# The expert stage of a two-block transformer kernel: last units in one pass, output as [token, channel], elementwise work moved off GpSimd

## The chip, the cores and the metric

The kernel runs on one core of a Trainium2 chip. The metric is the device time of one execution in microseconds (us), as the median of the runs. The kernel before takes 3832.88 us, the median of three runs from 3824.02 to 3834.84 us. TensorE (PE, with its weight loads as PEld) does the matmuls, VectorE (DVE), ScalarE (ACT) and GpSimd (POOL) the elementwise work, and SyncE (SP), ACT and POOL start DMAs. Each engine takes its instructions in the order of its own queue.

## The reference

The input has 512 tokens of 1,024 channels, in float32. The first block has two layers of gated feed-forward, token mixing and gated feed-forward again; the second has another token mixing with layer norm, and then a feed-forward of 16,384 experts, which is what the change is about:

```python
def peer_ffn(x, wq, sub_keys, u_tab, v_tab):      # x [512, 1024]
    q = (xf @ wq).reshape(t, 8, 2, 128)           # 8 heads, two half keys each
    scores = einsum("thpc,hpnc->thpn", q, sub_keys)          # 128 keys per half
    s_top, i_top = top_k(scores, 16)
    cand_s = s_top[:, :, 0, :, None] + s_top[:, :, 1, None, :]   # 16 x 16 sums
    best_s, best_pos = top_k(cand_s, 16)          # 16 experts per head and token
    gates = softmax(best_s)
    act = gelu(einsum("cd,chkd->chk", x, u_tab[expert_idx])) * gates
    return einsum("chk,chkd->cd", act, v_tab[expert_idx])

x = layer_norm(ALPHA * x + m, ln1_g, ln1_b)       # ALPHA = 2 ** 0.25
x = layer_norm(ALPHA * x + peer_ffn(x, ...), ln2_g, ln2_b)
```

The expert number is 128 times the index in the first half plus the index in the second. `u_tab` and `v_tab` are two tables of 16,384 rows of 1,024 numbers, 64 MB each.

## The kernel before, in words

Activations lie as eight tiles `x[k]` of [128 channels, 512 tokens]. Every matmul on weights is done with numbers split in a high and a low part in the type fp32r: three products, high by high (L262), high by low (L263) and low by high (L264). A weight unit of 128 x 1,024 floats is loaded by SP (`unit`, L246) into one of four buffers `raw`; ACT rounds it to `wh` (L249), and DVE or POOL subtracts to get `wl` (L250); `wh` and `wl` have three buffers each. `proj` (from L267) runs the eight blocks of a unit one after the other, three products each (`mm3`).

The method `peer` holds the expert stage. It treats the first 128 tokens in another way than the other 384.

- For the first 128 tokens the chosen rows of both tables are fetched. For each of the 128 places (8 heads by 16) POOL starts an indirect DMA (L1733) of one row of `u_tab` per token; DVE multiplies it by the token and sums (L1717). Then one row of `v_tab` per token is fetched, and DVE adds it to `vacc` with its weight (L1725). These are 256 gathers of 0.5 MB, dealt out over the stage by `ROW_STEPS`.
- For the other 384 tokens all experts are computed, 128 units of 128 experts. In stage 1 each unit is a `proj` with `pu`, then gelu on ACT, and the [128, 384] result goes to a buffer `HS` in device memory, with a store from SP (L1787).
- Beside these units runs `route`, dealt out at `ROUTE_STEPS` steps per unit: queries (16 units of `wq`, three of them begun earlier), scores in plain F32 (L1604), the two rounds of top 16 on DVE (`top16`), and `resolve` (equality on DVE, L1573; multiply on POOL, L1576; sum on DVE, L1579). Then for each of six blocks of 64 tokens the gates are spread over all experts by outer products. For four tokens at a time: DVE writes one-hot rows `o1` (L1665) and `o2` (L1667); ACT (four instructions, L1672) and POOL (L1669) scale `o2` with the high and the low part of the gate into `og`; PE multiplies (L1679, 256 columns, two banks for four tokens, from a ring of four banks); ACT copies the high half into `st` (L1683) and DVE adds the low half (L1684). SP stores `st` into a buffer `G`; the last block stays in SBUF.
- In stage 2 each of the 128 units is loaded from `pv`, `HS` and `G`. POOL multiplies activation and gate (`weighted`, L1813 and L1815), ACT and DVE split the product (L257, L258), and PE adds 24 matmuls of 384 columns into eight banks, one per tile of 128 channels.
- At the end `vacc` is added by transposing matmuls, the mean over channels is taken by matmuls with ones, and eight tiles [128 channels, 512 tokens] are stored; the host transposes them.

What sets the order: the code is emitted in program order, except that `issue_after(self.latest)` puts the dealt-out work of routing and rows on each engine right behind the last `wl` on DVE. Each engine's queue is then fixed.

Of the kernel before, what the change touches and what calls it, by code (L numbers as in the profile page):

```python
# [10 lines left out]
F32 = mybir.dt.float32  # L11
# [33 lines left out]
ROWS = 6  # L45


ROUTE_STEPS = 1.65
ROW_STEPS = (1.5, 0.9, 1.0)
# [87 lines left out]
def _layout(inp):  # L137
# [42 lines left out]
    a["ln"] = np.stack([_cols(inp[k][0]) for k in ("ln1_g_2", "ln1_b_2", "ln2_g_2", "ln2_b_2")], 1)  # L180
# [8 lines left out]
class Net:  # L189
    def __init__(self, tc, A, es):  # L190
# [9 lines left out]
        self.evn = 0  # L200
        c = self.const
        self.ident = c.tile([P, P], F32, name="ident")
# [8 lines left out]
        for i in range(2):  # L211
            nc.vector.tensor_copy(self.mdiag[:, i * P:(i + 1) * P], md[:, :P])
        self.x = [c.tile([P, S], F32, name=f"x{k}") for k in range(KT)]

# [272 lines left out]
    def start(self):  # L487
# [17 lines left out]
        self.gain = c.tile([P, DEPTH, 3, KT], F32, name="gain")  # L505

# [1033 lines left out]
    def resolve(self, best, pos, itop, ii, h0, nh):  # L1540
# [27 lines left out]
        for q in range(nh // 2):  # L1568
            for side in range(2):
# [6 lines left out]
                nc.gpsimd.tensor_tensor(e4, e4, it4[:, 2 * q:2 * q + 2, side, None, :].to_broadcast([P, 2, 16, 16]),  # L1576
# [5 lines left out]
    def route(self, X, G, begun):  # L1582
# [53 lines left out]
        for n, (t, a, b) in enumerate(BLOCKS):  # L1636
# [4 lines left out]
            if t not in numbers:  # L1641
# [7 lines left out]
                gh = self.blk(F32R, name="gh")  # L1649
                self.split(tr[:, 2 * P:3 * P], gh[:, :P], gh[:, P:2 * P])  # L1650
                trb = gh[:, 2 * P:].bitcast(BF)[:, :P]
                nc.vector.tensor_copy(trb, tr[:, P:2 * P])
                numbers[t] = tr, gh.bitcast(F32), trb
                yield
            tr, ghf, trb = numbers[t]
# [43 lines left out]

    def four(self, dt, name):  # L1700
        return self.stage.tile([P, 1024], dt, name=name, tag="four", bufs=4)

    def chosen(self, XN, acc):
# [33 lines left out]
        while flying:  # L1737
            land()
            yield True

    def peer(self, out, begun):
        nc, A = self.nc, self.A
        self.next_phase(24, {"A": 3, "S": 1, "T": 4})
# [147 lines left out]
```

## Time and profile before

| | |
|---|---|
| median of the runs | 3832.88 us |
| the profiled execution | 3826.24 us |
| its span | 3824.3 us |
| PE busy | 3582.7 us, 94% |
| DVE busy | 2617.1 us, 68% |
| ACT busy | 1532.2 us, 40% |
| POOL busy | 1162.6 us, 30% |
| DMA | 648.92 MB, mean 170 GB/s |

The span is the time from the first to the last event of one profiled execution, taken with a hardware profiler. Busy times are the union of an engine's instructions; a matmul's record lasts longer than its share of the pipeline, so records overlap. The granted clock (PEclk) is the share of the full clock of 2.4 GHz that PE was given; the other level is 1.2 GHz. Waits are put down to the instruction whose signal came last.

### The profile page before, as it was taken

To read this page: it belongs to the slowest core of one execution; us is meant where nothing else is said; L and a number is where in the kernel's file an instruction comes from. 1 tells how busy PE (TensorE), PEld (TensorE's weight loads), DVE (VectorE), ACT (ScalarE), POOL (GpSimd) and SP (SyncE) were. 2 spreads that over 40 slices of the span, in tenths; PEclk is the share of its full clock that TensorE was granted. 3 is DMA by queue.
4 is the path that set the end of the run, shared out by engine and by line. 5 is a ranking of instruction groups with operands and counts; after the bars stand their busy time and mean duration, and the time that the engine had idled before them with its cause. 6 is when DMAs were issued, how large, how long until landed. Compare 5 with 4: busy or idle time off the path is not lost. (4 is left out here: it accounts for less than half of the span.)

```text
span 3824.3 us, 50711 instructions
## 1 busy us (share of the span) xinstructions
PE 3582.7 (94%) x18689; PEld 3117.3 (82%) x18689; DVE 2617.1 (68%) x4588; ACT 1532.2 (40%) x2751; POOL 1162.6 (30%) x963
## 2 busy tenths in 40 slices
PE   7999999999999999999999989899788888999996
PEld 6888876788888888768888877788788788999996
DVE  6554687655563324876332485689999999999997
ACT  4222366322232223564322353433456466333332
POOL 0000310100010002101000132466676676776664
PEclk9999999999999999999999999999899899999998
DMA  7655320266643333301333222476676777999994
GB/s 244 189 183 184 123 72 12 94 201 190 195 152 99 93 97 104 106 17 45 105 94 93 90 69 70 147 227 220 190 251 236 245 243 255 352 340 341 340 339 141
DMA packets 230329, 648.92 MB, mean 170 GB/s; under 512 B 22784, under 2 KB 80304, under 8 KB 227520
## 3 DMA queue, kind: packets, MB, share of 16 engines
q1 hardware_dynamic: 190592, 506.20, 40.7%
q0 software_dynamic: 39488, 139.48, 10.8%
q8 instruction: 146, 2.39, 0.3%
q14 instruction: 103, 0.84, 0.1%
HBM read 597.36 MB, written 48.23 MB: 169 GB/s over the span
## 5 line engine op out<-in xcount | busy, mean ns | idle before, releaser
L264 PE MATMUL proj<-yh,wl 128*128 128x512 f32 (+2 forms) x3296 | 1208.8, 368 | 55.3 <-DVE wl L250 37.0
L249 ACT ACTIVATE wh<-raw 128x1024 fp32r<-128x1024 f32 (+2 forms) x622 | 648.3, 1043 | 1440.7 <-PE proj L263 793.1
L262 PE MATMUL proj<-yh,wh 128*128 128x512 f32 (+2 forms) x3296 | 1203.9, 370 | 17.4 <-DVE cc L1483 8.8
L263 PE MATMUL proj<-yl,wh 128*128 128x512 f32 (+2 forms) x3296 | 1209.0, 368 | 6.0 <-DVE yl L380 3.4
L250 DVE TENSOR_TENSOR wl<-raw,wh 128x1024 fp32r<-128x1024 f32 (+2 forms) x527 | 708.1, 1345 | 507.3 <-ACT wh L249 500.4
L264 PEld LDWEIGHTS proj<-yh,wl 128*128 128x128 f32 x3296 | 633.1, 192 | 146.9 <-DVE wl L250 45.6
L262 PEld LDWEIGHTS proj<-yh,wh 128*128 128x128 f32 x3296 | 628.7, 193 | 104.6 <-DVE cc L1483 8.9
L263 PEld LDWEIGHTS proj<-yl,wh 128*128 128x128 f32 x3296 | 633.3, 192 | 86.2 <-DVE yl L380 6.5
L393 POOL TENSOR_TENSOR acc<-acc,sq 128x512 f32<-128x512 f32 x32 | 48.9, 1528 | 1545.5 <-ACT sq L392 1176.8
L262 PE MATMUL acc<-yh,wh 128*128 128x384 f32 x1024 | 344.5, 337 | 0.4 <-ACT yh L257 0.4
L263 PE MATMUL acc<-yl,wh 128*128 128x384 f32 x1024 | 344.4, 336 | 0.1
L264 PE MATMUL acc<-yh,wl 128*128 128x384 f32 x1024 | 343.9, 336 | 0.5 <-DVE wl L250 0.5
L262 PE MATMUL proj<-gh,wh 128*128 128x512 f32 (+1 forms) x792 | 294.9, 372 | 1.1 <-ACT wh L249 1.1
L264 PE MATMUL proj<-gh,wl 128*128 128x512 f32 (+1 forms) x792 | 292.7, 370 | 2.5 <-DVE wl L250 2.5
L263 PE MATMUL proj<-gl,wh 128*128 128x512 f32 (+1 forms) x792 | 293.4, 370 | 0.0
L250 POOL TENSOR_TENSOR wl<-raw,wh 128x1024 fp32r<-128x1024 f32 x95 | 239.1, 2519 | 98.3 <-ACT wh L249 97.6
L518 DVE SCALAR_TENSOR_TENSOR scr<-raw,cact 128x1024 bf16<-128x1024 f32 x128 | 156.7, 1225 | 148.0 <-DMA raw<-in_wada 147.4
L1725 DVE SCALAR_TENSOR_TENSOR vacc<-row,act,vacc 128x1024 f32<-128x1024 f32 x127 | 213.5, 1681 | 0.4
L1733 POOL DMA_INDIRECT row<-in_purows,c x128 | 151.1, 1180 | 196.5 <-DVE row L1717 124.7
L1733 POOL DMA_INDIRECT row<-in_pv,c x128 | 149.5, 1168 | 154.6 <-DVE vacc L1725 72.2
L1717 DVE SCALAR_TENSOR_TENSOR row<-row,cact 128x1024 f32<-128x1024 f32 x128 | 187.4, 1480 | 11.7 <-DMA row<-in_purows,c 11.6
L262 PEld LDWEIGHTS acc<-yh,wh 128*128 128x128 f32 x1024 | 192.4, 188 | 1.0 <-ACT yh L257 0.7
(436 smaller groups left out, 5138.3 us busy)
## 6 DMA issues: line engine op xcount, KB each, us to landing
raw<-in_wada SPq DMA_DIRECT2D x144, 512.0 KB
raw<-in_pu SPq DMA_DIRECT2D x128, 512.0 KB
raw<-in_pv SPq DMA_DIRECT2D x128, 512.0 KB
raw<-in_wg SPq DMA_DIRECT2D x84, 512.0 KB
raw<-in_wu SPq DMA_DIRECT2D x84, 512.0 KB
raw<-in_wd SPq DMA_DIRECT2D x64, 512.0 KB
acts<-hg SPq DMA_DIRECT2D x128, 192.0 KB
hs<-acts SPq DMA_DIRECT2D x64, 384.0 KB
```

What stands on the lines that cost most here:

```text
L249: nc.scalar.activation(h[:, :n], raw[:, :n], AF.Copy)
L250: ins = (engine or nc.vector).tensor_sub(l[:, :n], raw[:, :n], h[:, :n].bitcast(F32))
L262: mm(out, lhsT=lh, rhs=rh, start=start, stop=False)
L263: mm(out, lhsT=lh, rhs=rl, start=False, stop=False)
L264: mm(out, lhsT=ll, rhs=rh, start=False, stop=stop)
L393: (engine or nc.vector).tensor_add(acc[:, s], acc[:, s], sq)
L518: nc.vector.scalar_tensor_tensor(scr, raw, 1.0, self.cact, op0=OP.mult, op1=OP.mult, accum_out=self.mod[:, l, j:j + 1])
L1717: nc.vector.scalar_tensor_tensor(row, row, 1.0, XN, op0=OP.mult, op1=OP.mult, accum_out=a)
L1725: nc.vector.scalar_tensor_tensor(acc, row, a, acc, op0=OP.mult, op1=OP.add)
L1733: nc.gpsimd.indirect_dma_start(out=row, out_offset=None, in_=tables[kind], in_offset=bass.IndirectOffsetOnAxis(ap=self.experts[:GT, s:s + ...
```

## The change

- `proj` runs pass by pass: eight products of `wh` with the high parts, eight of `wh` with the low parts, then eight of `wl`.
- All `wl` of the expert units are made by DVE, and the multiply in `resolve` too. POOL keeps the gathers, a few loads and six adds at the end.
- The gates' outer products are plain F32 matmuls of 128 columns, with `og` written by ACT alone; four tokens share one bank, and one ACT instruction copies it out. The low half, its POOL multiply and DVE's add are gone.
- `ROUTE_STEPS` is 2.3 instead of 1.65. Routing ends after 92 units (`kept`), whose activations go to `HS`, now with a store from ACT's queue. The last 36 units are fused: `proj`, gelu, multiply by the gates from `G` (DVE), split, and the second product, one unit behind. The 92 units from `HS` follow, loaded in pairs, multiplied and split 768 wide by DVE.
- The second product takes the activations as the stationary operand and the weights as the moving one, so that it gives [token, channel]: 18 matmuls of 512 columns per unit into six banks.
- The layer norm at the end is done per tile of 128 tokens (`finish`), with sums along the free dimension, and needs x as [token, channel]: 32 transposes instead of 8 (`XT`). The scales `ln2` are loaded as broadcast rows by POOL. The output is stored as [512, 1024].
- `pad` fills the pools in SBUF, so that each begins at a multiple of 512 bytes. `ROWS`, the buffers of gathered rows, is 5 instead of 6, and `ROW_STEPS` deals out other numbers of rows: 75 fall into stage 1, 93 into the fused units and 88 into the late ones, where it was 129 or 130 in stage 1 (124 of them behind 2424 us) and the rest in stage 2.

```diff
-ROUTE_STEPS = 1.65
-ROW_STEPS = (1.5, 0.9, 1.0)
+ROUTE_STEPS = 2.3
+ROW_STEPS = (1.2, 0.8, 2.6, 1.0)
...
+    def pad(self, pool, name, n):
+        self.nc.vector.memset(pool.tile([P, n], F32, name=name, bufs=1), 0.0)
...
-            for k in range(m):
-                xh, xl = X[c + k]
-                s = slice(k * P, (k + 1) * P)
-                self.mm3(ps, h[:, s], l[:, s], xh, xl, c + k == 0, c + k == nk - 1)
+            for i, (w, part) in enumerate(((h, 0), (h, 1), (l, 0))):
+                for k in range(m):
+                    self.nc.tensor.matmul(ps, lhsT=w[:, k * P:(k + 1) * P], rhs=X[c + k][part], start=c + k + i == 0,
+                                          stop=i == 2 and c + k == nk - 1)
...
-                nc.gpsimd.tensor_tensor(e4, e4, it4[:, 2 * q:2 * q + 2, side, None, :].to_broadcast([P, 2, 16, 16]),
+                nc.vector.tensor_tensor(e4, e4, it4[:, 2 * q:2 * q + 2, side, None, :].to_broadcast([P, 2, 16, 16]),
...
-                ot = o2.rearrange("p e t -> p t e")
-                nc.gpsimd.tensor_tensor(og[:, :, 1], ot, ghf[:, P + q:P + q + 4, None].to_broadcast([P, 4, P]),
-                                        op=OP.mult)
                 for i in range(4):
-                    nc.scalar.activation(og[:, i, 0], ot[:, i], AF.Copy, scale=ghf[:, q + i:q + i + 1])
+                    nc.scalar.activation(og[:, i * P:(i + 1) * P], o2[:, :, i], AF.Copy,
+                                         scale=tr[:, 2 * P + q + i:2 * P + q + i + 1])
 
                 def outer(o1=o1, og=og, q=q):
-                    for u in range(2):
-                        ps = self.bank("gp", "T")
-                        for i in range(2):
-                            v = u * 2 + i
-                            nc.tensor.matmul(ps[:, i * 256:(i + 1) * 256], lhsT=o1[:, v * P:(v + 1) * P],
-                                             rhs=og[:, v].rearrange("p a b -> p (a b)"), start=True, stop=True)
-                        p4 = ps.rearrange("p (t x e) -> p e t x", t=2, x=2)
-                        v = q - a + u * 2
-                        nc.scalar.activation(st[:, :, v:v + 2], p4[:, :, :, 0], AF.Copy)
-                        nc.vector.tensor_tensor(st[:, :, v:v + 2], st[:, :, v:v + 2], p4[:, :, :, 1], op=OP.add)
+                    ps = self.bank("gp", "T")
+                    for i in range(4):
+                        c = slice(i * P, (i + 1) * P)
+                        nc.tensor.matmul(ps[:, c], lhsT=o1[:, c], rhs=og[:, c], start=True, stop=True)
+                    nc.scalar.activation(st[:, :, q - a:q - a + 4], ps.rearrange("p (t e) -> p e t", t=4), AF.Copy)
...
+        def second(h, l, hi, lo, end, t):
+            for i, (a, w) in enumerate(((hi, h), (lo, h), (hi, l))):
+                for m in range(2):
+                    q = 2 * t + m
+                    nc.tensor.matmul(acc[q], lhsT=a[:, t * P:(t + 1) * P], rhs=w[:, m * S:(m + 1) * S],
+                                     start=q not in started, stop=end and i == 2)
+                    started.add(q)
...
+        while not over or kept % 2:
+            g = self.t32("hg")[:, GT:]
+            activations(kept, g)
+            nc.scalar.dma_start(HS[kept // 2, :, kept % 2], g)
+            over = over or routed(ROUTE_STEPS)
             gather(ROW_STEPS[self.known == P])
+            kept += 1
...
+        for j in range(kept, NE):
+            if j % 2 == 0:
+                g4 = gates(stage.tile([P, 2 * n], F32, name="gs", tag="gs"), j)
+            hs = self.blk(name="hs")[:, :n]
+            activations(j, hs)
+            nc.vector.tensor_mul(hs.rearrange("p (b t) -> p b t", t=BT), hs.rearrange("p (b t) -> p b t", t=BT),
+                                 g4[:, :, j % 2])
+            hi, lo = (v[:, :n] for v in self.new_pair())
+            self.split(hs, hi, lo)
+            fused.append((*self.unit(A["pv"][:, j]), hi, lo))
+            gather(ROW_STEPS[2])
+            if len(fused) > 1:
+                both(fused.pop(0))
...
+        for j in range(0, kept - 2, 2):
+            for i, hl in enumerate(weighted(j)):
+                both((*self.unit(A["pv"][:, j + i]), *hl))
+                if not self.gathered:
+                    gather(ROW_STEPS[3])
+                    if self.gathered:
+                        finish(0, [vacc[:, :S], vacc[:, S:]])
...
+        for t in range(NT - early):
+            for i, e in enumerate(ends):
+                second(*e, i == 1, t)
+            finish(early + t, acc[2 * t:2 * t + 2])
```

DVE's queue in the middle of the gates, before: `o_...<-pcst,tr` and `o_...<-iota,gh` are the one-hot rows, `st<-st,gp` the add of the low half, `vacc<-row` a gathered row.

```order
L1667 TENSOR_TENSOR o_25934<-iota_19121,gh 128x512
L1667 TENSOR_TENSOR o_25944<-iota_19121,gh 128x512
L250 TENSOR_TENSOR wl<-raw,wh 128x1024
L1725 SCALAR_TENSOR_TENSOR vacc<-row,act,vacc 128x1024 x2
L1667 TENSOR_TENSOR o_25991<-iota_19121,gh 128x512
L1665 TENSOR_TENSOR o_26044<-pcst,tr 128x512
L1684 TENSOR_TENSOR st<-st,gp 128x128x2 x2
L1665 TENSOR_TENSOR o_26064<-pcst,tr 128x512
L1667 TENSOR_TENSOR o_26045<-iota_19121,gh 128x512
L1667 TENSOR_TENSOR o_26065<-iota_19121,gh 128x512
L1684 TENSOR_TENSOR st<-st,gp 128x128x2 x2
L1665 TENSOR_TENSOR o_26121<-pcst,tr 128x512
```

Of each four tokens two adds stand here, among the one-hot rows, the rows and every second unit's `wl` (the others are POOL's).

The same part after (L1674 and L1676 are the one-hot rows, L1724 a row, L259 `wl`):

```order
L1674 TENSOR_TENSOR o_22757<-pcst,tr 128x512
L259 TENSOR_TENSOR wl<-raw,wh 128x1024
L1724 SCALAR_TENSOR_TENSOR vacc<-row,act,vacc 128x1024
L259 TENSOR_TENSOR wl<-raw,wh 128x1024
L1674 TENSOR_TENSOR o_22772<-pcst,tr 128x512
L1674 TENSOR_TENSOR o_22821<-pcst,tr 128x512
L1676 TENSOR_TENSOR o_22822<-iota_19129,tr 128x512
L1676 TENSOR_TENSOR o_22837<-iota_19129,tr 128x512
L1724 SCALAR_TENSOR_TENSOR vacc<-row,act,vacc 128x1024
L1676 TENSOR_TENSOR o_22889<-iota_19129,tr 128x512
L1676 TENSOR_TENSOR o_22904<-iota_19129,tr 128x512
L259 TENSOR_TENSOR wl<-raw,wh 128x1024
```

The adds L1684 have left the queue, and `wl` of the units stands more often in it.

PE's queue at the gates, before:

```order
L264 MATMUL proj<-yh,wl 128x384
L262 MATMUL proj<-yh,wh 128x384
L263 MATMUL proj<-yl,wh 128x384
L264 MATMUL proj<-yh,wl 128x384
L1679 MATMUL gp<-og,o_23778 128x256 x4
L1679 MATMUL gp<-og,o_23835 128x256 x4
L262 MATMUL proj<-yh,wh 128x384
L263 MATMUL proj<-yl,wh 128x384
L264 MATMUL proj<-yh,wl 128x384
L262 MATMUL proj<-yh,wh 128x384
```

The three products alternate, and the outer products stand between two blocks.

And after (L283 is the projection, L1685 the outer products):

```order
L283 MATMUL proj<-yh,wh 128x384 x8
L283 MATMUL proj<-yl,wh 128x384 x8
L283 MATMUL proj<-yh,wh 128x384 x8
L283 MATMUL proj<-yl,wh 128x384 x4
L1685 MATMUL gp<-og,o_22559 128x128 x2
L283 MATMUL proj<-yl,wh 128x384
L1685 MATMUL gp<-og,o_22559 128x128 x2
L283 MATMUL proj<-yl,wh 128x384 x3
L1685 MATMUL gp<-og,o_22568 128x128 x4
L283 MATMUL proj<-yh,wh 128x384 x2
L283 MATMUL proj<-yh,wl 128x384 x8
```

The three products of a block no longer alternate, and the outer products of four tokens, now of 128 columns, stand inside a pass.

PE's queue in the fused units, after; there is no such place before (L1806 is the second product):

```order
L283 MATMUL proj<-yh,wh 128x384 x8
L283 MATMUL proj<-yl,wh 128x384 x8
L283 MATMUL proj<-yh,wl 128x384 x8
L1806 MATMUL acc<-wh,yh 128x512 x2
L1806 MATMUL acc<-wh,yl 128x512 x2
L1806 MATMUL acc<-wl,yh 128x512 x2
L1806 MATMUL acc<-wh,yh 128x512 x2
L1806 MATMUL acc<-wh,yl 128x512 x2
L1806 MATMUL acc<-wl,yh 128x512 x2
```

Each projection is followed by the 18 products of the unit before it, two per stationary operand.

## Rows read from the trace of the kernel before

**Rows 1.** Table of stages: window, length, busy of PE, PEld, DVE, ACT, POOL, PEclk, DMA share, GB/s.
```profile
0.00:2391.00 2391.00, 2299.56 (x11561) 1871.26 (x11562) 1326.55 (x2392) 898.79 (x1550) 223.08 (x219) 0.98 0.37 117
...
2424.00:2738.00 314.00, 275.00 (x1467) 255.60 (x1466) 273.96 (x1061) 105.17 (x147) 193.24 (x113) 0.96 0.66 213
2738.00:3246.00 508.00, 436.17 (x2414) 426.22 (x2413) 478.54 (x621) 300.35 (x755) 351.33 (x234) 0.94 0.72 243
3246.00:3784.00 538.00, 537.12 (x3104) 535.95 (x3104) 499.45 (x452) 204.03 (x264) 369.61 (x382) 1.00 0.94 328
3784.00:3824.30 40.30, 7.43 (x34) 6.98 (x32) 22.82 (x43) 7.98 (x12) 13.55 (x10) 0.53 0.14 52
```

**Rows 2.** The same table for two windows of 100 us with PE always busy.
```profile
200.00:300.00 100.00, 100.00 (x439) 82.05 (x438) 53.98 (x73) 28.27 (x35) 0.00 (x0) 1.00 0.62 194
3400.00:3500.00 100.00, 100.00 (x579) 100.00 (x578) 93.53 (x81) 38.12 (x48) 68.61 (x72) 1.00 0.97 338
```

**Rows 3.** PE's waits, 2424 to 3246 us: sum in us, times, longest.
```profile
PE gp L1679 <- DVE st L1684: 51.9, 28, 5.5
PE proj L264 <- DVE wl L250: 33.3, 11, 12.3
PE proj L264 <- POOL wl L250: 16.7, 8, 6.1
PE gp L1679 <- POOL og L1669: 8.7, 3, 3.2
```

**Rows 4.** Timeline of PE at a score matmul: start, length, operation.
```profile
2446.69 1.05 PE L1604 MATMUL sc<-keys,x 128*128 128x128 f32 x8
2447.50 0.42 PE L262 MATMUL proj<-yh,wh 128*128 128x384 f32 x1
```

**Rows 5.** DVE's operations by form, 2424 to 3246 us: busy, mean ns, idle before.
```profile
L1665 DVE TENSOR_TENSOR o<-pcst,tr 128x512 fp32r<-128x512 f32 x96 | 133.7, 1401 | 1.8 <-PE gp L1679 1.8
L1717 DVE SCALAR_TENSOR_TENSOR row<-row,cact 128x1024 f32<-128x1024 f32 x77 | 118.8, 1568 | 11.7 <-DMA row<-in_purows,c 11.6
L250 DVE TENSOR_TENSOR wl<-raw,wh 128x1024 fp32r<-128x1024 f32 x62 | 94.3, 1524 | 11.5 <-ACT wh L249 11.4
L1725 DVE SCALAR_TENSOR_TENSOR vacc<-row,act,vacc 128x1024 f32<-128x1024 f32 x47 | 80.1, 1704 | 0.3
L1684 DVE TENSOR_TENSOR st<-st,gp 128x256 f32<-128x256 f32 x192 | 74.7, 435 | 6.0 <-ACT st L1683 5.9
L1667 DVE TENSOR_TENSOR o<-iota,gh 128x512 bf16<-128x512 bf16 x96 | 64.7, 692 | 0.0
```

**Rows 6.** DVE's timeline around 2472 us and from 2749 to 2766 us.
```profile
2471.78 1.22 DVE L250 TENSOR_TENSOR wl<-raw,wh 128x1024 fp32r<-128x1024 f32 x1
2472.91 0.40 DVE L1534 MAX8 x<-cand 128x8 f32<-128x88 f32 x2
...
2749.37 2.74 DVE L250 TENSOR_TENSOR wl<-raw,wh 128x1024 fp32r<-128x1024 f32 x1
...
2754.32 0.41 DVE L1667 TENSOR_TENSOR o<-iota,gh 128x512 bf16<-128x512 bf16 x1
...
2766.05 0.68 DVE L1665 TENSOR_TENSOR o<-pcst,tr 128x512 fp32r<-128x512 f32 x1
```

**Rows 7.** POOL's operations by form, 2424 to 3246 us.
```profile
L250 POOL TENSOR_TENSOR wl<-raw,wh 128x1024 fp32r<-128x1024 f32 x78 | 197.8, 2539 | 25.9 <-ACT wh L249 25.2
L1669 POOL TENSOR_TENSOR og<-o,gh 128x512 fp32r<-128x512 bf16 x96 | 121.5, 1275 | 29.5 <-DVE o L1667 22.7 <-PE proj L264 4.0 <-PE gp L1679 1.8
```

**Rows 8.** Timeline of the end: last matmuls, first and last small operation, stores.
```profile
3783.75 0.38 PE L1834 MATMUL acc<-ident,vacc 128*128 128x128 f32 x2
...
3799.21 0.16 DVE L1256 TENSOR_SCALAR lnm<-stat 128x4 f32<-128x4 f32 x1 [3.12 <-PE stat L1253]
...
3802.05 0.16 DVE L1267 TENSOR_TENSOR lnmr<-lnm,rsy 128x4 f32<-128x4 f32 x1
...
3808.81 6.68 SPq L1841 DMA_DIRECT2D out<-y  x8
```

More of the change, by code (lines that the diff above doesn't have):

```diff
@@ L201, in __init__ @@
         c = self.const
+        self.pad(c, "pad0", 96)
         self.ident = c.tile([P, P], F32, name="ident")
@@ L1739, in chosen @@
             yield True
+        self.gathered = True
     def peer(self, out, begun):
         nc, A = self.nc, self.A
-        self.next_phase(24, {"A": 3, "S": 1, "T": 4})
+        self.phase.close()
         self.stage = self.phase.enter_context(self.tc.tile_pool(name="stage", bufs=1))
-        G = self.dram.tile([P, len(BLOCKS) - 1, NE, BT], F32, name="gates")
-        HS = self.dram.tile([NE // 2, P, 2, S - GT], F32, name="acts")
-        cst = self.blk(name="pcst")
+        stage = self.stage
+        blocks = self.phase.enter_context(ExitStack())
+        self.pools(blocks, 22, {"A": 3, "S": 1, "T": 4})
+        n, last, early = S - GT, len(BLOCKS) - 1, GT // P
+        G = self.dram.tile([P, last, NE, BT], F32, name="gates")
+        HS = self.dram.tile([NE // 2, P, 2, n], F32, name="acts")
+        cst = stage.tile([P, S], F32, name="pcst", tag="pcst")
         self.iota, self.tv, self.ti = cst[:, :P], cst[:, P:P + 128], cst[:, 256:384].bitcast(U32)
@@ new lines, in both, with gates, activations @@
+        def both(args, end=False):
+            for t in range(NT - early):
+                second(*args, end, t)
+        def gates(tile, j):
+            g4 = tile.rearrange("p (b i t) -> p b i t", i=2, t=BT)
+            nc.sync.dma_start(g4[:, :last], G[:, :, j:j + 2])
+            nc.scalar.activation(g4[:, last], self.last_gates[:, j:j + 2], AF.Copy)
+            return g4
+        def activations(j, g):
+            ps = self.proj(A["pu"][j], dense, n=n)
+            nc.scalar.activation(g, ps, AF.Gelu_apprx_tanh)
@@ new lines, in peer @@
+        kept, over = 0, False
+        while not over or kept % 2:
[3 more added lines that the diff above has]
+            over = over or routed(ROUTE_STEPS)
+            gather(ROW_STEPS[self.known == P])
+            kept += 1
+        self.kept = kept
+        acc += [self.bank("acc", t) for t in "TTTTSA"]
+        fused, g4 = [], None
+        for j in range(kept, NE):
[11 more added lines that the diff above has]
+                both(fused.pop(0))
@@ new lines, in peer, with two @@
+        for f in fused:
+            both(f)
+        blocks.close()
+        late = self.phase.enter_context(self.tc.tile_pool(name="late", bufs=1))
+        row = [self.x[i] for i in range(4)]
+        for i in range(4):
+            src = A["ln2"][i // 2, i % 2 * S:(i % 2 + 1) * S]
+            nc.gpsimd.dma_start(row[i], bass.AP(tensor=src.tensor, offset=src.offset, ap=[[0, P], [1, S]]))
+        def two(name, dt=F32, bufs=5):
+            return late.tile([P, 2 * n], dt, name=name, tag=name, bufs=bufs)
@@ new lines, in weighted, with finish @@
+        def weighted(j):
+            hs = two("hs")
+            nc.sync.dma_start(hs.rearrange("p (i t) -> p i t", i=2), HS[j // 2])
+            g4 = gates(two("gq"), j)
+            h4 = hs.rearrange("p (i b t) -> p b i t", i=2, t=BT)
+            nc.vector.tensor_mul(h4, h4, g4)
+            hi, lo = two("hi", F32R, 2), two("lo", F32R, 2)
+            self.split(hs, hi, lo)
+            return [(hi[:, i * n:(i + 1) * n], lo[:, i * n:(i + 1) * n]) for i in range(2)]
+        def finish(t, halves):
+            y = stage.tile([P, D], F32, name="row", tag="row", bufs=ROWS)
+            parts, sq = self.sm(2, "fsum"), self.sm(2, "fsq")
+            for m, v in enumerate(halves):
+                c = slice(m * S, (m + 1) * S)
+                nc.vector.scalar_tensor_tensor(y[:, c], XT[t][:, c], ALPHA, v, op0=OP.mult, op1=OP.add,
+                                               accum_out=parts[:, m:m + 1])
+            mean, var = self.sm(1, "fmean"), self.sm(1, "fvar")
+            nc.vector.scalar_tensor_tensor(mean, parts[:, :1], parts[:, 1:], self.negd, op0=OP.add, op1=OP.mult)
+            scr = stage.tile([P, D], F32, name="row", tag="row", bufs=ROWS)
+            nc.scalar.activation(scr, y, AF.Square, bias=mean, accum_out=sq[:, :1])
+            nc.vector.tensor_scalar(var, sq[:, :1], 1.0 / D, LN_EPS, op0=OP.mult, op1=OP.add)
+            r = self.rsqrt(var, 1)
+            mr = self.sm(1, "fmr")
+            nc.vector.tensor_mul(mr, mean, r)
+            for m in range(2):
+                c = slice(m * S, (m + 1) * S)
+                nc.scalar.activation(y[:, c], y[:, c], AF.Identity, scale=r, bias=mr)
+                nc.vector.tensor_mul(y[:, c], y[:, c], row[m])
+                (nc.vector if t == NT - 1 else nc.gpsimd).tensor_add(y[:, c], y[:, c], row[2 + m])
+                nc.sync.dma_start(out[t * P:(t + 1) * P, c], y[:, c])
@@ new lines, in peer @@
+        self.negd = self.sm(1, "negd", bufs=1)
+        nc.vector.memset(self.negd, -1.0 / D)
+        for j in range(0, kept - 2, 2):
[5 more added lines that the diff above has]
+                        finish(0, [vacc[:, :S], vacc[:, S:]])
+        ends = [(*self.unit(A["pv"][:, kept - 2 + i]), *hl) for i, hl in enumerate(weighted(kept - 2))]
@@ L1844, in program @@
+        if not self.gathered:
+            for _ in rows:
+                pass
+            finish(0, [vacc[:, :S], vacc[:, S:]])
+        for t in range(NT - early):
+            for i, e in enumerate(ends):
+                second(*e, i == 1, t)
+            finish(early + t, acc[2 * t:2 * t + 2])
 def program(tc, A, out):
```

108 lines of the change are left out of this document (33 added, 75 removed).

## The prediction, made before the changed kernel ran

> **What bounds the kernel now.** I read the table of stages first [rows 1], then two windows of 100 us [rows 2], PE's waits in the expert stage [rows 3], the operations of DVE and POOL there [rows 5 to 7], and the end [rows 8]. Seen in the table: up to 2391 us PE is busy 96% of the time; from 3246 to 3784 us (stage 2) it is busy 537 of 538 us. Between them, from 2424 to 3246 us (stage 1, routing and gates beside 127 units), it is busy 275.0 + 436.2 = 711 of 822 us, so 111 us idle, and its granted clock is 0.96 and 0.94 where stage 2 has 1.00. Nearly all room is there, and in the 40 us after the last matmul.
>
> How much stage 1 loses follows from PE's price at full clock. 100 us hold 439 matmuls of 512 columns, 0.2278 us each, or 579 of 384 columns, 0.1727 us each [rows 2]. Stage 1 has 127 units of 24 x 0.1727 = 4.145 us (526 us), 13 query units of 24 x 0.2278 (71), 384 gate matmuls of 256 columns at half of 0.2278 (44) and 64 score matmuls in plain F32. Four of those, eight records, take between 0.81 us (to the start of the next matmul) and 1.05 us [rows 4], so 0.20 to 0.26 each; I take 0.22, in sum 14. That is 655 us. 822 - 655 = 167 us are lost: 111 idle, and 56 in which PE counts as busy but runs slower or restarts.
>
> The idle time is four waits [rows 3]: the gate matmuls for DVE's add into st, which frees their bank (51.9), for POOL's og (8.7), and the third product for wl, from DVE (33.3) or POOL (16.7). Behind three of the four stands DVE, 274.0 + 478.5 = 752 of 822 us busy. Part of that is not work. The same subtraction for wl takes 1.13 us from start to start at 2471.78, and 2.74 us at 2749.37 [rows 6]; the mean of 62 is 1.524 [rows 5]. The other operations are stretched likewise: L1665 0.68 against 1.401, L1667 0.41 against 0.692. POOL does elementwise work in this stage, 197.8 us of wl and 121.5 of og [rows 7].
>
> By the Trainium skill (SBUF — State Buffer, section on the two separate sides), DVE and GpSimd share a port pair as an exclusive lock for a whole instruction. The stretched rows agree, 2.74 against 1.22 us. The same section speaks against this change: DVE operations in a two-port mode keep GpSimd from writing descriptors. Each gather would then be held by one DVE operation, about 1.2 us; POOL has little else to do in 1,290 us and 256 gathers, so by that the sum would stay, unless rows come late. No run here shows it yet.
>
> **The change, part by part.**
>
> Stage 1, DVE. L1684 goes (74.7 us). With no elementwise POOL work the prices fall to the undisturbed ones (0.08 of a duration overlaps the next): wl 62 x (1.524 - 1.13) = 24, L1665 96 x (1.401 - 0.60) = 77, L1667 96 x (0.692 - 0.34) = 34, rows 77 x (1.568 - 1.17) + 47 x (1.704 - 1.17) = 56; together 191. Rows, 1,024 wide like wl, I price at 1.17 with their accumulator read. There are 75 instead of 124: -57. All wl now fall to DVE, 92 + 13 = 105 instead of 62: +49. The multiply of L1576 comes over, 32 x 0.60 = +19. 752 - 75 - 191 - 57 + 49 + 19 = 497 us.
>
> Stage 1, PE. 92 units remain here (381 us), the query units (71), the scores (14), 384 gate matmuls in F32 at 0.22 (85, between 77 and 100 by the bounds above), and 24 more transposes for the token-major copy of x at 0.2 to 0.3 (7). In sum 558 us. DVE's 497 fits below it, 80% of the stage where it was 92%.
>
> What is still lost is the choice that weighs most. Of the four waits st and og lose their cause, 60.6 us, and so do POOL's wl, 16.7. DVE's wl (33.3 in 11 waits) stays, but pass by pass the first wl is used 16 matmuls after the first wh instead of 2: 14 x 0.1727 = 2.4 us later. That is worth at most 11 x 2.4 = 27, so 7 to 33 remain. New: the gates now wait for ACT's four copies and its one evacuation, and wl stands behind pieces of routing that come at 2.3 per unit instead of 1.65. I take 40 us idle, and 20 of the 56 for slow running, which follows idle time. Bounds: 0 (stage 2 shows it: 1 us idle in 538) and the 167 of before. Stage 1 = 558 + 60 = 618 us instead of 822.
>
> The stores of HS move from SP to ACT, 92 issues. Eight stores of the end take 6.68 us on their queue, paced by their data [rows 8], so 0 to 0.83 us each, at most 76 us on an engine that is busy 405 us in this stage [rows 1] and loses 35 wh. I take nothing: a wh that is 0.8 us late is under the 2.4 us that wl has won. Up to 2391 us pass order only moves waits at the start of a projection: 0, with 6 us either way.
>
> Fused units. 36 units of 24 x 0.1727 + 18 x 0.2278 = 8.245 us: 297 us. DVE has two wl, 93 / 36 = 2.6 rows, a multiply and a subtraction per unit: 2 x 1.13 + 2.6 x 1.17 + 2 x 0.5 = 6.3 us. The chain gelu, multiply, high part, low part is four operations of at most 0.7 us and has the 8.2 us of another unit as cover, since the second products come one unit later.
>
> Late units. 92 x 18 x 0.2278 = 377 us (4.100 each, against 4.145). DVE per unit: wl, 88 / 92 of a row and half of a 768-wide multiply and subtraction, about 3.2 us. DMA is at a share of 0.94 in stage 2 [rows 1], 0.97 in a calm part, at 338 GB/s [rows 2]. A late unit moves 0.52 MB of weight, 0.36 of activations and gates and 0.50 of gathered rows: 1.39 MB in 4.10 us is 338 GB/s, the same rate. So it may be a bound: at the 328 of [rows 1] it is 4.23 us, +12 for the stage. I take 377.
>
> By the Trainium skill (DMA: Bandwidth & Descriptors, section on how a descriptor splits into AXI transactions), a descriptor that starts off a multiple of 256 bytes costs one transaction more: 17 for 4,096 bytes, 16 once pools start at multiples of 512. By it the late stage keeps 377 us; without it up to 389. No row of before shows it.
>
> By the Trainium skill (TensorE: Matmul & The Clock Gate, section on 56 and 53.3 ns), back-to-back matmuls cost N / 2.4 plus 2.5 ns, so the gain from 384 to 512 columns would be 0.015 us per unit, 2 us in all; the rows give 0.045, 6 us. The rows decide; the sum would differ by 4.
>
> The end. From 3784.1 us (last matmul) to 3824.3 it is 40.2 us: per-channel sums by matmul, 12 small operations, spread by matmul, eight outputs, and 8.8 us after the last issue at 3815.5 [rows 8]. Now every token tile ends by itself, two under the last matmuls. Left is one tile: two adds with sums (1.5), mean, a square of 1,024 (1.1), the small chain of 3 us (3799.21 to 3802.05), then three operations per half at about 0.7, some 10 to 11 us, and 8.8: 20 us, so 20 less. For the change of stages, with its banks passed over, I leave 4 us.
>
> **Sum.** 2424 + 618 + 297 + 377 + 4 + 20 = 3740 us of span, +1.9 as in the profiled execution (3826.24 against 3824.3): 3742. The median of the runs is 3832.88, 6.6 above that execution, so 3749 us: 84 less than before. By terms: losses -107, gates in F32 +41, transposes +7, 512 columns -6, end -20.
>
> **Rivals.**
> Slower: DVE's order, not its load, holds PE in stage 1. Its queue is in order, routing is dealt out in pieces of 40 to 80 instructions, each piece now holds up the only engine that makes wl, and the pace is higher. For it: a wait for DVE's wl lasted up to 12.3 us [rows 3], five times what pass order gives back. Against it: 191 us of stretching goes. If the stage loses the old 167 us, the dearer gates and the transposes decide: 3742 + 107 + 6.6 gives 3856. It is slower than before from a loss of 144 on, by more than 0.3% from 155.
> No change: a loss of 144, or fused units whose chain is 2.3 us late each (36 x 2.3 = 83): 3833. Against the second: the 8.2 us of cover.
> DMA holds the fused and late units: +12 there, and 36 x 0.4 in the fused ones (2.6 rows, two weights and gates, 2.6 MB in 8.2 us, 315 GB/s): about 3775.
> More gain: with DVE at 80% and no port shared the stage loses 20 or less, as stage 2 does: 3705.
>
> **How the numbers follow.** The forecast, 3749, has 0.53; more gain, 3705, 0.17; DMA, 3775, 0.10; no change 0.09; slower, 3856, 0.11. 0.3% (11.5 us) is about what a measurement tells from no change. So faster 0.80, same 0.09, slower 0.11. The forecast alone reaches from 3715 to 3790 (idle 10 to 75, gates -8 to +15, first part 6 either way); 8 in 10 need 3685 to 3825.
>
> **What would show it.** Right: wl near 1.2 us wherever PE works, a granted clock near 1.0 in stage 1, waits of gp gone, stage 1 near 620 us, fused units at 8.2 us and late ones at 4.1 with PE idle under 1%, 20 us after the last matmul. Wrong: PE's waits for wl or og above 100 us in stage 1, DVE above 95% there, late units at 4.2 with wh waiting for raw, rows that wait for gathers.

## The result, and the profile after

The changed kernel takes 3734.68 us (median of four runs, 3732.47 to 3735.86). Its ratio to the kernel before, which with a fourth run has a median of 3833.86 us, is 0.9742, 95% interval 0.9718 to 0.9765: 2.6% faster, 14 us under the forecast of 3749 and inside the range. The profiled execution has a span of 3732.2 us, 92 less than before. The table of stages after has the columns of [rows 1]. Its second row is stage 1 (routing beside 92 units), the third the fused units, the fourth the late ones, the last the end:

```profile
0.00:2374.00 2374.00, 2284.12 (x11563) 1875.09 (x11564) 1323.93 (x2398) 914.24 (x1550) 218.03 (x219) 0.98 0.37 118
...
2408.00:3013.00 605.00, 576.21 (x3427) 555.79 (x3426) 495.18 (x1484) 356.39 (x733) 113.43 (x87) 0.97 0.68 232
3013.00:3306.00 293.00, 293.00 (x1483) 266.62 (x1482) 229.06 (x286) 114.58 (x163) 127.33 (x92) 1.00 0.89 308
3306.00:3711.50 405.50, 387.66 (x1666) 311.72 (x1664) 299.02 (x345) 142.54 (x192) 111.62 (x84) 0.99 0.88 304
3711.50:3732.20 20.70, 0.00 (x0) 0.00 (x0) 14.04 (x45) 5.58 (x8) 6.41 (x4) 0.61 0.20 76
```

Against the forecast: stage 1 605 us (618), fused units 293 (297), late ones 405 (377, and 4 for the change of stages), the end 20.7 (20), and the part up to 2374 us, of which nothing was expected, about 17 us shorter. The fused units and the end were near and stage 1 was 13 us better. Two terms were off by some 20 us, in opposite directions: the first part and the late units. Of the 92 us, the part before stage 1 gives 16, stage 1 and the second products together 56, the end 20. No run takes back the end alone; its 20 us are read from the two traces.

The next rows are PE's waits in stage 1, which answer to [rows 3]. The four sums there, 110.6 us, have become 29 us of idle time, of which these four rows are 25:

```profile
PE proj L283 <- DVE wl L259: 13.8, 5, 4.3
PE gp L1685 <- ACT og L1678: 5.2, 6, 1.8
PE proj L283 <- ACT hg L1823: 4.2, 4, 2.5
PE gp L1685 <- DVE wl L259: 2.1, 1, 2.1
```

DVE's operations in the same stretch answer to [rows 5]. The stretching is gone: they take what the undisturbed ones took in [rows 6].

```profile
L259 DVE TENSOR_TENSOR wl<-raw,wh 128x1024 fp32r<-128x1024 f32 x105 | 127.8, 1220 | 79.1 <-ACT wh L258 67.8 <-PE proj L283 10.9 <-issue 0.3
L1674 DVE TENSOR_TENSOR o<-pcst,tr 128x512 f32<-128x512 f32 x96 | 65.4, 685 | 10.4 <-PE gp L1685 10.1
...
L1676 DVE TENSOR_TENSOR o<-iota,tr 128x512 bf16<-128x512 bf16 x96 | 37.1, 421 | 9.6 <-issue 5.6 <-DMA acts<-hg 4.0
```

In the first part PE's pace itself has changed. The window of [rows 2] from 200 to 300 us holds 443 matmuls of 512 columns, where it was 439:

```profile
200.00:300.00 100.00, 100.00 (x443) 82.81 (x442) 53.58 (x74) 29.32 (x35) 0.00 (x0) 1.00 0.61 191
```

From one start to the next, a matmul takes 227 ns after; before, the three alternating products took 226, 229 and 232 ns.

The late units lose PE time in two places. The first is where they begin. PE's timeline there (start, length, operation):

```profile
3307.52 0.61 PE L1806 MATMUL acc<-wl,yh 128*128 128x512 f32 x2
3318.00 1.22 PE L1806 MATMUL acc<-wh,hi 128*128 128x512 f32 x2 [9.86 <-ACT hi L266]
3319.02 1.20 PE L1806 MATMUL acc<-wh,lo 128*128 128x512 f32 x2
```

SP starts the first load of `hs` at 3308.17 us, behind the last fused product, whose buffers the new pool takes over; PE stands still for 9.9 us and then runs at the lower clock until 3323 (a granted clock of 0.50 from 3318 to 3323 us). The second place comes back 12 times:

```profile
PE acc L1806 <- DVE lo L267: 7.5, 12, 1.2
```

DVE's timeline in one such pair, and PE's wait there:

```profile
3384.54 0.96 DVE L1866 TENSOR_TENSOR hs<-hs,gq 128x768 f32<-128x768 f32 x1 [2.96 <-DMA hs<-acts]
3385.41 1.22 DVE L259 TENSOR_TENSOR wl<-raw,wh 128x1024 fp32r<-128x1024 f32 x1
3386.55 0.95 DVE L267 TENSOR_TENSOR lo<-hs,hi 128x768 fp32r<-128x768 f32 x1
```
```profile
3387.55 0.73 PE L1806 MATMUL acc<-wh,lo 128*128 128x512 f32 x2 [0.80 <-DVE lo L267]
```

The multiply that waits for its load belongs to a later pair; `lo`, which PE needs now, stands behind it in DVE's queue.

### The profile page after: what moved, and what is told of

The parts are those of the page before. It is cut to its first block, busy times and chain, and to the rows that moved or that the text cites. A ratio compares the mean times of both kernels' runs of the same rounds, so it can differ in the third digit from the quotient of the medians.

```text
span 3732.2 us, 48937 instructions
## 1 busy us (share of the span) xinstructions
PE 3569.3 (96%) x18265; PEld 3032.3 (81%) x18265; DVE 2377.8 (64%) x4577; ACT 1552.6 (42%) x2675; POOL 583.7 (16%) x490
## 4 chain that ended last, share of the span: by engine, by line
PE 38%; DVE 11%; DMA 7%; issue 2%; ACT 2%; SPq 0%; DVEq 0%; POOL 0%; ACTq 0%; POOLq 0%
PE proj L283 22%; PE acc L1806 7%; DMA hs<-acts 5%; DVE wl L259 3%; PE gp L1685 2%; DVE ch L1338 1%; DMA gates<-st 1%; PE proj L272 1%; PE proj L271 1%; PE proj L273 1%; DVE lo L267 1%; PE o L1085 1%; DVE row L1716 1%; PE tp L863 1%; ACT wh L258 0%
## 5 line engine op out<-in xcount | busy, mean ns | idle before, releaser
L259 DVE TENSOR_TENSOR wl<-raw,wh 128x1024 fp32r<-128x1024 f32 (+1 forms) x607 | 736.7, 1215 | 530.3 <-ACT wh L258 437.7
L283 PE MATMUL proj<-yh,wh 128*128 128x512 f32 (+1 forms) x2744 | 646.3, 376 | 18.3 <-DVE cc L1494 9.6
L283 PE MATMUL proj<-yh,wl 128*128 128x512 f32 (+1 forms) x2744 | 628.7, 371 | 13.8 <-DVE wl L259 13.8
L283 PE MATMUL proj<-yl,wh 128*128 128x512 f32 (+1 forms) x2744 | 628.7, 370 | 0.0
L283 PEld LDWEIGHTS proj<-yh,wh 128*128 128x128 f32 x2744 | 502.3, 190 | 94.1 <-DVE cc L1494 9.7
L283 PEld LDWEIGHTS proj<-yh,wl 128*128 128x128 f32 x2744 | 505.9, 189 | 83.2 <-DVE wl L259 15.8
L283 PEld LDWEIGHTS proj<-yl,wh 128*128 128x128 f32 x2744 | 505.6, 189 | 67.7
L272 PE MATMUL proj<-yl,wh 128*128 128x256 f32 (+1 forms) x552 | 179.1, 332 | 5.8 <-DVE yl L389 3.4
L1806 PE MATMUL acc<-wh,lo 128*128 128x512 f32 x552 | 174.2, 397 | 7.9 <-DVE lo L267 7.5
L1806 PE MATMUL acc<-wh,hi 128*128 128x512 f32 x552 | 171.2, 391 | 9.9 <-ACT hi L266 9.9
L273 PE MATMUL proj<-yh,wl 128*128 128x256 f32 (+1 forms) x552 | 177.1, 327 | 0.8 <-DVE wl L259 0.3
L271 PE MATMUL proj<-yh,wh 128*128 128x256 f32 (+1 forms) x552 | 168.3, 332 | 8.0 <-ACT yh L634 6.3
L1806 PE MATMUL acc<-wl,hi 128*128 128x512 f32 x552 | 171.2, 391 | 0.0
L1724 DVE SCALAR_TENSOR_TENSOR vacc<-row,act,vacc 128x1024 f32<-128x1024 f32 x127 | 162.5, 1280 | 0.6
L283 PE MATMUL proj<-gh,wl 128*128 128x512 f32 x616 | 153.3, 389 | 0.0
```

What stands on the lines that cost most here:

```text
L259: ins = (engine or nc.vector).tensor_sub(l[:, :n], raw[:, :n], h[:, :n].bitcast(F32))
L271: mm(out, lhsT=lh, rhs=rh, start=start, stop=False)
L272: mm(out, lhsT=lh, rhs=rl, start=False, stop=False)
L273: mm(out, lhsT=ll, rhs=rh, start=False, stop=stop)
L283: self.nc.tensor.matmul(ps, lhsT=w[:, k * P:(k + 1) * P], rhs=X[c + k][part], start=c + k + i == 0, stop=i == 2 and c + k == nk - 1)
L1724: nc.vector.scalar_tensor_tensor(acc, row, a, acc, op0=OP.mult, op1=OP.add)
```

## The experiments

Where each kernel spends its time, from its profile, in us: the start of the last statistics matmul before the expert stage; stage 1 from the first 384-column matmul to the first second product (this begins 4 us before the window above and ends 4 us behind it, with the first fused projection: 613 for 605); from there to the start of the last matmul; the span. The ratio is to the kernel before, executed again along with each, with its interval. Kernels with the same code in a part show what one profile's figure is worth: the first part ends between 2364.6 and 2370.1 us in eight kernels, routing at 1.7 steps among them, and the second products take 689.6 to 695.7 us in six whose edits lie elsewhere.

| kernel | first part | stage 1 | second products | span | ratio |
|---|---|---|---|---|---|
| before | 2385.6 | - | - | 3824.3 | 1 |
| changed | 2368.2 | 613.3 | 693.7 | 3732.2 | 0.9742 (0.9718-0.9765) |
| blocks alternate | 2377.1 | 645.7 | 693.7 | 3773.7 | 0.9851 (0.9829-0.9872) |
| no pads | 2410.4 | 614.8 | 701.4 | 3784.8 | 0.9889 (0.9872-0.9905) |
| activations 256 bytes off | 2368.1 | 614.8 | 692.8 | 3732.7 | 0.9748 (0.9729-0.9767) |
| weights 416 bytes off | 2411.8 | 613.2 | 700.3 | 3783.1 | 0.9890 (0.9871-0.9909) |
| before with pads | 2377.8 | - | - | 3819.4 | 0.9979 (0.9970-0.9989) |
| wl on POOL again | 2364.9 | 646.5 | 690.8 | 3759.8 | 0.9838 (0.9822-0.9854) |
| spare product on POOL | 2369.3 | 658.3 | 694.4 | 3779.0 | 0.9861 (0.9844-0.9877) |
| add on DVE | 2365.1 | 626.6 | 689.6 | 3738.3 | 0.9776 (0.9759-0.9793) |
| stores from SP | 2370.1 | 598.2 | 695.7 | 3720.9 | 0.9716 (0.9700-0.9732) |
| own buffer for the product | 2369.4 | 613.1 | 678.6 | 3717.9 | 0.9704 (0.9688-0.9721) |
| and first pair early | 2364.6 | 613.5 | 670.0 | 3705.2 | 0.9680 (0.9664-0.9696) |

**Blocks alternate.**
```diff
-            for i, (w, part) in enumerate(((h, 0), (h, 1), (l, 0))):
-                for k in range(m):
+            for k in range(m):
+                self.mm3(ps, h[:, s], l[:, s], xh, xl, c + k == 0, c + k == nk - 1)
```


> The changed kernel with the projections block by block again (the three products of a block alternate); pads stay. In the changed kernel the part before the expert stage ends 17 us earlier (last statistics matmuls at 2365.0 us instead of 2382.4), and a 512-column matmul takes 227 ns in each pass where the three alternating products took 226, 229 and 232 ns. Theory 1 (the order of the products does it): those three prices return, the part before 2374 us is 15 to 19 us longer, and stage 1 loses a further 10 to 27 us to waits for wl: in sum 25 to 46 us more than the changed kernel, 3760 to 3781. Theory 2 (the pads do it): 227 ns stays, the first part is within 3 us, and only the waits for wl in stage 1 return: 3745 to 3762.


Measured: 3774.23 us. The time lies where theory 1 put it, but not for its reason: all products stay at 226 to 227 ns. What holds of it are the waits. Stage 1 is 32 us longer, with this row where the changed kernel has 13.8:
```profile
PE proj L273 <- DVE wl L259: 37.8, 12, 9.3
```
The first part is 9 us longer. Waits for `wl` at the start of projections are 6.6 us there, 0.3 in the changed kernel.

**No pads.**
```diff
-        self.nc.vector.memset(pool.tile([P, n], F32, name=name, bufs=1), 0.0)
+        return
```


> The changed kernel without the pads: buffers start 256 or 416 bytes off a multiple of 512. Theory 1 (order): first part unchanged within 3 us, in sum within 5 us of the changed kernel (3730 to 3740). Theory 2 (pads): the first part is 15 to 19 us longer, in sum about 3752. The rule on transactions of DMA adds in either case: a late stage that is held by DMA gets longer by up to 5% of its DMA time, up to 20 us, if starts off a multiple of 256 bytes cost; raw at 416 is off it, the activations at 256 are not.


Measured: 3784.53 us, 50 more than the changed kernel and over what either theory gave. Of these, 42 us are in the first part, where matmuls now take 231 to 238 ns, more than the 229 of the kernel before on the mean, and 8 in the second products. The pads do it, and pass by pass suffers more without them: the change without its pads would have gained 1.1%. Of the dearer DMA transactions nothing is seen: a packet of 4,096 bytes takes 159 ns (median) in the kernel before, in the changed one and with weights 416 bytes off.

**Activations or weights off the line.** One size each:
```diff
-PAD = 40
+PAD = 104          # activations 256 bytes off, weights on the line
```
```diff
-PAD = 40
+PAD = 64           # and pad0 to pad2 left out: weights 416 off, activations on the line
```


> The changed kernel with the last pad 256 bytes longer: weights (raw, wh, wl) start at multiples of 512 bytes, the activations of the blocks 256 bytes off. Without any pads a 512-column matmul of a projection took 232 to 238 ns instead of 227 and the first part was 42 us longer. Theory A (the start of the moving operand, the activations in the projections): projections again at 232 or more, first part 35 to 45 us longer, the second products (moving operand: weights) at 227; in sum 3770 to 3782. Theory B (the start of the weights): all at 227, in sum 3730 to 3740. Theory C (the offset of the two against each other): both at other prices than 227, also the second products, 3775 to 3790.

> The changed kernel with the pads moved so that the activations start at multiples of 512 bytes and the weights 416 bytes off. Theory A (moving operand): projections at 227 ns, first part within 3 us of the changed kernel, the second products (moving: weights) at 231 to 238 ns, 2304 x 7 ns = 16 us at most; in sum 3735 to 3752. Theory B (weights): projections at 232 or more, first part 35 to 45 us longer, in sum 3770 or more. Theory C: both raised.


Measured: 3734.39 and 3787.68 us. Theories A and C fall with the first of the two (443 matmuls in the same window, second products at 227 ns). B holds for the projections; in the second products, where the weights move, weights off the line are dear as well (234 ns), so it is the weights in either role. (The three pads that were left out shift the constants ahead of the weights too, which these products don't read.) Two windows with the weights off the line, pass by pass, in the columns of [rows 2], have 430 and 500 matmuls where the changed kernel has 443 and 508:
```profile
200.00:300.00 100.00, 100.00 (x430) 80.47 (x429) 54.26 (x76) 28.18 (x34) 0.00 (x0) 1.00 0.59 187
3100.00:3200.00 100.00, 100.00 (x500) 90.37 (x499) 77.31 (x95) 38.41 (x55) 44.35 (x31) 1.00 0.89 311
```
Activations 416 bytes off and weights 256 off were not tried. The two offsets differ, so it stays open which divisor of 512 the weights need, and whether activations at 416 would cost.

**Before with pads.**
```diff
+        self.pad(c, "pad0", 96)    # pad1 64, pad2 120, in small 48
-ROWS = 6
+ROWS = 5
```


> The kernel before with pads so that all its buffers start at multiples of 512 bytes, and five buffers of gathered rows instead of six, since the pads don't fit otherwise; nothing else. Theory (the start of the weights sets the price of a matmul): products at 226 to 227 ns where they took 226, 229 and 232, the first part 7 to 10 us shorter as in the changed kernel with alternating products (2373.9 against 2382.4 us), stage 2 and the stage 1 within 5 us: 3815 to 3828. Rival (the start only hurts pass by pass): within 4 us of before.


Measured: 3820.95 us, 7 less than the 3828.33 of the kernel before executed along with it, as the theory had it. So the pads alone bring about a twelfth of the gain (0.0021 of 0.0258), and without them the pass order costs: the end of the first part is at 2385.6 us with neither, 2377.8 with pads alone, 2410.4 with pass order alone and 2368.2 with both.

**Work back on POOL.** `wl` and the multiply of `resolve`; in another kernel a product like the old `og`, which nothing reads:
```diff
-                nc.vector.tensor_tensor(e4, e4, ...
+                nc.gpsimd.tensor_tensor(e4, e4, ...
...
-            ps = self.proj(A["pu"][j], dense, n=n)
+            pool = not started and not acc and (self.known < P or j % 2 == 0)
+            ps = self.proj(A["pu"][j], dense, n=n, engine=nc.gpsimd if pool else None)
```
```diff
+                spare = self.blk(name="spare").rearrange("p (a b) -> p a b", b=P)
+                nc.gpsimd.tensor_tensor(spare, o2.rearrange("p e t -> p t e"), ..., op=OP.mult)
```


> The changed kernel with wl of every second stored unit (of all while the first tokens are routed) and the multiply in resolve on POOL again. Theory (the prediction): DVE's operations that overlap with POOL's are stretched again, wl on DVE from 1.22 to about 1.5 us, the one-hot rows from 0.68 to 1.0 or more, and PE waits for wl of POOL (2.5 us each): 20 to 60 us more, 3755 to 3795. Rival (the DVE queue has room, and shared ports cost only when DVE is full): DVE is relieved of some 60 operations and the time stays within 8 us of the changed kernel.

> The changed kernel with one POOL multiply of 512 elements more for every four tokens of the gates, the old low part of og, into a spare buffer that nothing reads (it also takes one of the 22 blocks each time). Theory (most of the rest of stage 1's gain is that DVE's operations are no longer stretched by POOL's): the one-hot rows and wl on DVE are stretched again in the gates, by 40 to 100 us in sum, and PE waits 15 to 45 us more: 3750 to 3780. Rival (DVE has the room, as the added 75 us in another run cost 5): within 8 us of the changed kernel.


Measured: 3764.30 and 3775.43 us. Stage 1 is 33 and 45 us longer, and both rivals fall. In the first kernel DVE's operations are stretched again (`wl` 1.40 us, the one-hot rows 0.97 and 0.53), but PE also waits 9.8 us for POOL's own `wl` of 2.4 us, so its 33 us are not stretching alone:
```profile
L1674 DVE TENSOR_TENSOR o<-pcst,tr 128x512 f32<-128x512 f32 x96 | 91.6, 966 | 19.4 <-PE gp L1685 19.4
```
```profile
PE proj L283 <- POOL wl L259: 9.8, 3, 6.4
```
DVE with the spare product:
```profile
L259 DVE TENSOR_TENSOR wl<-raw,wh 128x1024 fp32r<-128x1024 f32 x107 | 143.7, 1347 | 62.7 <-ACT wh L258 51.7 <-PE proj L283 9.9 <-issue 0.9
L1674 DVE TENSOR_TENSOR o<-pcst,tr 128x512 f32<-128x512 f32 x96 | 83.8, 880 | 8.7 <-POOL spare L1678 6.2 <-PE gp L1688 2.4
L1676 DVE TENSOR_TENSOR o<-iota,tr 128x512 bf16<-128x512 bf16 x96 | 73.2, 786 | 4.4 <-ACT wh L258 4.4
```
and PE's waits:
```profile
PE proj L283 <- DVE wl L259: 21.2, 10, 5.1
PE gp L1688 <- DVE o L1674: 13.3, 12, 3.3
PE gp L1688 <- ACT og L1681: 13.1, 12, 4.0
```
The 6.2 us behind `POOL spare` in DVE's second row are waits for the spare product itself, not stretching.

**Add on DVE.**
```diff
...
+                    for u in range(0, 4, 2):
+                        v = st[:, :, q - a + u:q - a + u + 2]
+                        nc.vector.scalar_tensor_tensor(v, p4[:, :, u:u + 2], 0.0, v, op0=OP.mult, op1=OP.add)
```


> The changed kernel with two more operations of 256 elements on DVE for every four tokens of the gates, which read the bank after ACT and add zero to st: DVE's load of the old adds (192 of about 0.4 us, 75 us) and the bank held until DVE comes to it. Theory (waits for banks behind DVE's queue were the largest loss): gp waits for st again, 30 to 60 us in sum, 3765 to 3795. Rival (the old waits came from stretched operations, not from the add): DVE at 94% of stage 1 without stretching still keeps up, under 15 us, below 3750.


Measured: 3739.20 us, with stage 1 13 us longer; the theory falls. The wait that was 51.9 us in [rows 3] is now:
```profile
PE gp L1685 <- DVE st L1690: 7.4, 2, 3.9
```
The spare product stretches DVE's work by about 75 us (107 x 0.13 + 96 x 0.20 + 96 x 0.37 + 48 x 0.14), as much as these adds are, and costs three times as much in stage 1. The likely reason: it lengthens the path to the product, `o2` to `og` to PE, on which the two waits above of 13 us each stand, while the add comes behind the product. This isn't shown apart: the spare product also takes one of the 22 blocks each time.

**Stores from SP.**
```diff
-            nc.scalar.dma_start(HS[kept // 2, :, kept % 2], g)
+            nc.sync.dma_start(HS[kept // 2, :, kept % 2], g)
```


> The changed kernel with the 92 stores of HS issued by SP again instead of ACT. Theory (the prediction's zero for this edit): within 4 us of the changed kernel. Rival: a store that waits for gelu in SP's queue holds up the loads of the weights behind it: 5 to 20 us more; or ACT, freed of the issues, gives wh earlier: 3 to 8 us less.


Measured: 3719.46 us, stage 1 15 us shorter. Both the zero and the first rival fall; the second had the direction and not the size. ACT's timeline in the changed kernel shows the price:
```profile
2807.87 0.49 ACT L1823 ACTIVATE hg<-proj 128x384 f32<-128x384 f32 x1 [0.33 <-PE proj L283]
2808.40 0.33 ACTq L1829 DMA_DIRECT2D acts<-hg  x1
2808.82 2.52 ACT L1678 ACTIVATE og<-o,tr 128x128 f32<-128x128 bf16 x8 [0.46 <-PE gp L1685]
```
From the end of gelu to the next ACT operation 0.46 us pass, 0.33 of them the issue. In 29 of the 92 places the next operation follows the store in this way, 0.39 to 0.46 us behind gelu; in the others something else stands between or ACT waits longer for another reason. With the stores on SP the next operation can start some 0.1 us before gelu ends (29 places). PE's idle time in stage 1 falls from 29 to 19 us, and half of that is its wait for the gates' copies, 5.2 us in the changed kernel, of which this is left:
```profile
PE gp L1685 <- ACT og L1678: 0.4, 1, 0.4
```

**Own buffer for the product, and the first pair early.**
```diff
-        def two(name, dt=F32, bufs=5):
+        def two(name, dt=F32, bufs=4):
...
-            nc.vector.tensor_mul(h4, h4, g4)
+            hm = two("hm", F32, 2)
+            nc.vector.tensor_mul(hm.rearrange("p (i b t) -> p b i t", i=2, t=BT), h4, g4)
...
```
```diff
+        for i in range(2):
+            hs, gs = self.x[4 + i][:, :n], self.x[6 + i][:, :n]
...
+            first.append((hi, lo))
         for f in fused:
```


> The changed kernel with the product of activation and gate in the late units written to a buffer of its own (two of them; loads have four buffers instead of five). Theory: in the changed kernel the multiply of a pair that comes four pairs later stands in DVE's queue before the low part of the next pair, and waits for its load of activations (80 us of DVE's waits), so PE waits for lo, some 12 us with the restarts; with two buffers the multiply can't run so far ahead and its load is issued earlier: waits for lo under 2 us, 8 to 14 us less, 3720 to 3727. Rival (DMA is the bound of the late stage, 324 GB/s): the wait moves to raw or wh and the time stays within 4 us.

> As a_hm, and the activations and gates of the first two late units are loaded into free tiles of x and split there while the fused units run. Theory: the 10 us at the change from fused to late units are the loads that can start only when the pool is free; two units of 4.1 us cover most of it: the wait of 9.9 us and the slow restart (2.7) shrink to 0 to 5 us, so 7 to 12 us less than a_hm, 3710 to 3718. Rival: the loads of the next pairs are as late as before, since DMA is full there, and the wait moves behind the two units: within 4 us of a_hm.


Measured: 3717.67 and 3707.00 us, 17 and a further 11 us less. The mechanisms are those of the theories; the first gain is a little over its 8 to 14. With the first edit no wait for `lo` is left; with both, PE's waits from 3000 us to its last matmul are:
```profile
PE acc L1806 <- ACT hi L266: 1.7, 1, 1.7
PE acc L1806 <- DVE lo L267: 0.4, 1, 0.4
```
The late products then take 380 us, near the 377 of the forecast. This version beats both kernels. With the stores on SP as well it wasn't run.

**Routing at 1.7 steps**, 124 units through memory.
```diff
-ROUTE_STEPS = 2.3
+ROUTE_STEPS = 1.7
```


> The changed kernel with routing at 1.7 steps per unit: some 126 units go to memory and only two are fused. Theory (fusing is no gain for PE, which pays the same per unit; it takes loads off the late stage): fused units cost 8.14 us for both products without waits, late ones 4.40 with theirs, so 34 more late units cost up to 34 x 0.3 = 10 us more, and routing that is spread thinner gives back up to 20 us in stage 1: 3725 to 3745. Rival (fused units carry the gain, since DMA bounds the late stage): 3755 or more.


Measured: 3742.10 us, ratio 0.9782 (0.9765 to 0.9798). The time lies inside the theory's range and below the rival's. But the run doesn't decide what the fused units are worth: its last matmul starts at 3690.8 us, 20 before that of the changed kernel, and then 47 us follow, since DVE adds gathered rows that were dealt out too late until 3709 us and the end comes behind them. It does show that the faster routing has a price: with 32 more units in it, stage 1 has 17 us of idle PE time where the changed kernel has 29.

## Why the prediction was right, and where it wasn't

- Where the loss was: right. Stage 1 lost 167 us by the forecast's count and was to lose 60; at the forecast's work of 558 us it lost 47, 29 of them idle (40). DVE's busy time, 495.2 us, was forecast as 497.
- That the sum came within 14 us is in part luck. The first part (16 us less than forecast) and stage 1 (13 less) made up for the late units (24 more). Another 6 us come from the step from span to median, for which the forecast took the 6.6 us of the kernel before; here it is 0.7.
- Why it went: partly right. Work on POOL, put back, costs 33 and 45 us with DVE's operations stretched again, though neither run has the stretching alone. The order of the products is worth 32 us in stage 1, over the 27 that were called the most. The weight given to the add behind the gates was wrong: put back, it costs 13. Of the 51.9 us of [rows 3] the adds alone explain little; stretched operations ahead of them and two banks for four tokens are left as causes, and the banks weren't tried alone.
- Gates in F32, fused units: right. A gate matmul takes 0.224 us, in two records of 0.112 (0.22 was forecast), and no fused unit waited: PE is busy 293 of 293 us.
- "Up to 2391 us pass order only moves waits at the start of a projection: 0": this step failed, and with it the 6 us either way. It is 17 us, some 8 from the pads (before with pads 2377.8 against 2385.6) and 9 from the order, each give or take some us. The pads were costed as an affair of DMA alone; they set the pace of PE, and without them the order would have cost 25.
- "I take nothing" for stores from ACT failed: 15 us, within the bound of 76. The cover that it named, the 2.4 us that `wl` had won, doesn't help the gates' copies on the same engine.
- "I take 377" and "I leave 4 us" failed, by 24 us together. The DMA rival (+12) named the stage but not the mechanism: with its own buffer for the product the stage runs 15 us faster on the same bytes. It was an order in DVE's queue, and loads that wait for a pool.
- The doubt whether DVE holds up the gathers: it didn't show as a wait. An issue on POOL took 1.35 us on the mean where it was 1.17, and DVE waited for no gathered row (11.6 us before).
- The end: right in sum, 20.7 us. The list by terms leaves out the 4 us for the change of stages, one unit more behind stage 1 (4 us) and 7 us of old stage 2 that were no unit's; they nearly cancel.
- The slower rival fell: the longest wait for `wl` is 4.3 us where it was 12.3. Of the signs of being right, one came only in part: the granted clock in stage 1 is 0.97, not near 1.0.

## What to carry to other kernels

Take the loss of a stage from its idle time and its clock, and look for the engine behind the waits. In two runs some 75 us of DVE time cost 45 us as stretched operations ahead of a matmul and 13 as adds behind one: ask on which path an operation stands. Check where tiles start: the matmul price read from the trace of before held only for the starts and the order of that kernel. When work runs ahead in an in-order queue, ask which load it may wait for and what stands behind it.

## What was not expected of the hardware

- A 512-column matmul took 227 ns with weights at a multiple of 512 bytes and 231 to 238 with weights 416 bytes off, pass by pass; 256 bytes off made no difference for activations.
- Operations of DVE on 128 x 1 beside POOL's adds in the end took 1.2 us instead of 0.16. Four of them stand in the chain of the last tile, so some 4 of the 20.7 us at the end:
```profile
3716.24 6.41 POOL L1891 TENSOR_TENSOR row<-row,x 128x512 f32<-128x512 f32 x4 [19.30 <-DVE rsy L330]
...
3718.49 1.21 DVE L329 TENSOR_TENSOR rst<-rst,rsy 128x1 f32<-128x1 f32 x1
```
